# Packing the 256-column chunk of a SwiGLU FFN, and reordering the work around it, in a two-layer decoder trunk

## The chip, the cores and the metric

The kernel runs on one core of one Trainium2 chip. The metric is the device time of one execution in microseconds (us). The engines are called as the profile calls them: PE is TensorE's matmuls, PEld its weight loads, DVE is VectorE, ACT is ScalarE, POOL is GpSimd and SP is SyncE, whose queue issues nearly all DMAs.

## The reference

Two layers of a decoder on 256 positions of width 1024, in fp32. The first layer mixes with a causal gated MLP, the second with a sparse attention of three branches. In both layers the output of the mixer and that of a cross-attention into 256 memory positions are joined and projected, and a SwiGLU FFN of 2816 columns follows:

```python
for i in range(DEPTH):
    h = rmsnorm(x, norm_mix[i]);  mem_n = rmsnorm(mem, norm_mem[i])
    mix, mem_q = gmlp_mixer(h, ...) if i % 2 == 0 else nsa_mixer(h, ...)
    mem_o = mem_cross_attention(mem_q, mem_n, w_mem_kv[i])
    x = x + jnp.concatenate([mix, mem_o], axis=-1) @ w_out
    h = rmsnorm(x, norm_ffn[i])
    x = x + (jax.nn.silu(h @ wg) * (h @ wu)) @ wd
return rmsnorm(x, norm_final)
```

## The kernel before

**Products.** Every fp32 operand of a large product is split into two fp32r parts, high and low: for a weight piece `wH` (a cast on ACT, L123) and `wL` (a subtraction on DVE, L124), for an activation `aH` and `aL` in the same way. `mm3` then issues three matmuls, H·H (L229), L·H (L230) and H·L (L231); such three are called a triple below. The 256 positions are two blocks `tb` of 128. A `gemm` runs the eight 128-row slices of a weight against one block, eight triples into one PSUM tile; `down` runs some slices of a 1024-column weight into `accs[tb][half]`, four PSUM tiles of 512 columns that hold a layer's sum.

**Weights.** All weights pass through one stream: a `Raw` tile is loaded by SP (three buffers), cut into pieces of 1024 columns, and each piece is cast and subtracted into a `wH` and a `wL` of seven buffers. `AHEAD = 7` pieces may be live. A piece is released by `done()` when its last triple is issued, which lets the next be split, and a raw tile is loaded when the pieces of the one three places before it are split. So the order of the calls in the program sets the order of the loads.

**Order.** PE's order is the order of the calls. Between triples `Flow.tick` advances a model clock, and runs generators whose due time (a `spawn` delay or a `yield`) has come; these put transposes and small matmuls between triples. The other engines' instructions are placed by a scheduler, with priorities for what is in a `step`.

**PSUM.** Four tiles `mm` and four tiles `tr`, one bank of 512 columns each. `tr` tiles go round: an instruction that takes one waits until the readers of the tile four places back are done.

**Where the change touches.**

- `ffn_weights` and `ffn` (L429 to L470): the columns are taken as one chunk of 256 and five of 512. In the chunk of 256 the order is `gate(0)`, `up(0)`, `gate(1)`, `up(1)`, each eight triples of 256 columns, and then `down` with two slices. `gate` ends in a silu on ACT (L449), `up` spawns `turn`: the product with the silu on DVE (L453), 1.6 model us later two or four transposes, and the split into `act`, from which `down` reads.
- Layer 1's projection (L695 to L707): `mem_attention` (L382) is spawned for both blocks, the second 5.5 model us after the first. It makes scores (L389), a softmax over DVE, POOL and ACT, `MEMLAT = 9` model us later transposes and two copies on ACT (L414), and 3.2 later the product with the values (L422). The generator `v_chain` transposes the gated product `gm` into the other slices. `down` runs slices 0 to 3, and once both memory blocks are emitted slices 4 to 7 of both blocks.
- Layer 2's attention (L921 to L1073), for six head groups `m`: `scores(m)` leaves probabilities, `turn(m)` transposes them (L973 to L982) and at its end the compressed branch's `pcs` (L984, "tr<-ident,pcx" in the profile, with a copy on ACT at L985), `attend(m)` multiplies with the values (L1003) and splits the result into `mix1`. `mixed((m, tb))` is a `down` of one slice and one block, two triples. All of them stand in a written-out order.
- The end (`final`, L1081): after each 512-column half of a block, the residual (DVE, L307), a sum of squares (ACT, L250), the product with the final norm's weights (DVE, L1087); after a block's second half its factor on POOL (L258, L259) and the two scalings (DVE L1094, ACT L1096), each followed by a DMA of SP (L1097).

Of the kernel before, what the change touches and what calls it, by code (L numbers as in the profile page):

```python
# [12 lines left out]
ALU = mybir.AluOpType  # L13
# [48 lines left out]
MEMLAT = 9.0  # L62
# [6 lines left out]
def body(tc, t, out):  # L69
    nc = tc.nc  # L70
    PE, ACT, DVE, POOL, SP = nc.tensor, nc.scalar, nc.vector, nc.gpsimd, nc.sync
    with ExitStack() as ctx:
# [236 lines left out]
        def down(accs, act, ks, ws, first, last, after=None, tbs=(0, 1)):  # L309

            for tb in tbs:
                for half in range(2):
                    acc = accs[tb][half]
                    for i, k in enumerate(ks):
                        mm3(acc, st(act, k, tb), ws[i](slice(half * 512, (half + 1) * 512)),
                            first and i == 0, last and i == len(ks) - 1)
                        if tb == 1 and half == 1:
                            ws[i].done()
# [110 lines left out]
        def ffn_weights(layer):  # L429
            wg, wu, wd = t["ffn_w_gate"][layer], t["ffn_w_up"][layer], t["ffn_w_down"][layer]  # L430
            out = []
            for c0, n in [(2560, 256)] + [(i * 512, 512) for i in range(5)]:
                out.append((n // 128, w_in(wg, c0, n), w_in(wu, c0, n),
# [3 lines left out]
        def ffn(weights, nrm, after):  # L437
            accs = [[mm(), mm()], [mm(), mm()]]
            for ci, (nk, wg, wu, wd) in enumerate(weights):
                n = nk * 128  # L440
                sil = [None, None]
                act = mid([128, 4, SEQ], F32R), mid([128, 4, SEQ], F32R)

                def gate(tb):
                    ps = tr()
                    gemm(ps, nrm.act, tb, wg, n)
                    sil[tb] = small([128, n])
                    with tc.high_priority(offset=HI):
                        ACT.activation(sil[tb], ps[:, :n], AF.Silu, scale=nrm.rstd[tb])  # L449
# [19 lines left out]
                down(accs, act, range(nk), wd, ci == 0, last, end if last else None)  # L469
# [180 lines left out]
        def v_chain():  # L650
# [17 lines left out]
            for c, n in ((0, 512), (512, 256)):  # L668
                for tb in range(2):
# [4 lines left out]
                    yield 1.0  # L674
# [23 lines left out]
        for tb in range(2):  # L698
            flow.spawn(mem_attention(qT0, tb, kv0, mix, mo_done), 1.0 + 5.5 * tb)
# [270 lines left out]
        def turn(m):  # L970
# [169 lines left out]
```

## Time and profile before

| | us |
|---|---|
| device time, median of 3 runs (lowest, highest) | 633.94 (633.56, 634.37) |
| the profiled execution's own device time | 634.55 |
| its span, first to last instruction | 632.8 |
| PE busy | 618.1 (98%) |
| DVE busy | 377.1 (60%) |
| ACT busy | 327.3 (52%) |
| POOL busy | 58.2 (9%) |
| share of the chain that ended last: PE, ACT, DVE | 90%, 5%, 2% |
| share of 16 DMA engines on the weight queue | 51.9% |

PE's records are pipelined: one begins before the one ahead has ended. So a matmul's price is the distance of its start from the start of the next, and a wait is what such a distance has beyond the usual one. The mean granted clock of the profiled execution was 0.998.

### The profile page before, as it was taken

What the parts mean: (1) busy time and instruction counts of PE and PEld (TensorE: products, weight loads), DVE (VectorE), ACT (ScalarE), POOL (GpSimd) and SP (SyncE); (2) the same over time, 40 slices, a digit from 0 to 9 for tenths busy, and PEclk for the clock granted to TensorE, in tenths of its full rate; (3) what the DMA queues carried; (4) which work ended last, traced back from release to release, by engine and by line L of the source; (5) the groups of instructions that cost most, each with busy time, mean ns of one, the idle gap of its engine ahead of it and who ended that gap; (6) DMA issues with size and microseconds to landing.
All of it is one profiled execution on the core that took longest, in us unless ns stands there. A gap on an engine that the chain in (4) does not pass through costs nothing.

```text
span 632.8 us, 8848 instructions
## 1 busy us (share of the span) xinstructions
PE 618.1 (98%) x3382; PEld 513.9 (81%) x3382; DVE 377.1 (60%) x616; ACT 327.3 (52%) x553; POOL 58.2 (9%) x90
## 2 busy tenths in 40 slices
PE   8999999999999999999999999899999999999995
PEld 7889879888888888889886787678988888888884
DVE  3998457464554544566688479766544645446344
ACT  4885557452534434456543559766533535344423
POOL 0330121000000000002001204431000000000001
PEclk9999999999999999999999999999999999999999
DMA  7966254555546464643967742133554655647401
GB/s 244 369 217 247 75 165 169 200 172 186 177 171 225 138 261 134 241 159 87 330 201 206 193 103 65 35 121 115 198 199 134 226 173 179 220 138 235 159 1 67
DMA packets 57331, 109.69 MB, mean 173 GB/s; under 512 B 3429, under 2 KB 19401, under 8 KB 57289
## 3 DMA queue, kind: packets, MB, share of 16 engines
q1 hardware_dynamic: 57272, 109.12, 51.9%
q8 instruction: 26, 0.43, 0.3%
q14 instruction: 17, 0.13, 0.1%
q10 hardware_dynamic: 16, 0.00, 0.0%
HBM read 108.07 MB, written 1.05 MB: 172 GB/s over the span
## 4 chain that ended last, share of the span: by engine, by line
PE 90%; ACT 5%; DVE 2%; DMA 1%; issue 1%; POOL 0%; SPq 0%; POOLq 0%; ACTq 0%; DVEq 0%
PE mm L229 14%; PE mm L230 14%; PE mm L231 14%; PE tr L230 13%; PE tr L231 13%; PE tr L229 13%; PE tr L245 5%; ACT mid L951 3%; PE tr L800 1%; DMA x<-in_x_dram 1%; PE tr L389 1%; PE tr L422 1%; PE tr L1003 1%; ACT wH L123 1%; DVE wL L124 0%
## 5 line engine op out<-in xcount | busy, mean ns | idle before, releaser
L124 DVE TENSOR_TENSOR wL<-raw,wH 128x1024 fp32r<-128x1024 f32 (+1 forms) x170 | 205.5, 1228 | 149.5 <-ACT wH L123 143.8
L123 ACT CAST wH<-raw 128x1024 fp32r<-128x1024 f32 (+1 forms) x170 | 173.8, 1043 | 152.3 <-PE tr L230 75.5
L229 PE MATMUL tr<-wH,aH 128*128 128x512 f32 (+1 forms) x384 | 143.8, 375 | 0.0
L230 PE MATMUL tr<-wH,aL 128*128 128x512 f32 (+1 forms) x384 | 142.8, 372 | 0.6 <-DVE aL L124 0.6
L231 PE MATMUL tr<-wL,aH 128*128 128x512 f32 (+1 forms) x384 | 142.7, 372 | 0.0
L229 PE MATMUL mm<-wH,aH 128*128 128x512 f32 (+2 forms) x224 | 87.7, 391 | 0.0
L230 PE MATMUL mm<-wH,aL 128*128 128x512 f32 (+2 forms) x224 | 83.2, 371 | 0.0
L231 PE MATMUL mm<-wL,aH 128*128 128x512 f32 (+2 forms) x224 | 83.2, 371 | 0.0
L230 PEld LDWEIGHTS tr<-wH,aL 128*128 128x128 f32 x384 | 72.4, 188 | 13.0 <-DVE aL L124 0.9
L231 PEld LDWEIGHTS tr<-wL,aH 128*128 128x128 f32 x384 | 72.3, 188 | 12.5
L229 PEld LDWEIGHTS tr<-wH,aH 128*128 128x128 f32 x384 | 72.3, 188 | 12.3
L229 PE MATMUL mm<-wH,mid 128*128 128x512 f32 (+1 forms) x208 | 79.2, 381 | 0.0
L230 PE MATMUL mm<-wH,mid 128*128 128x512 f32 (+1 forms) x208 | 77.9, 374 | 0.0
L231 PE MATMUL mm<-wL,mid 128*128 128x512 f32 (+1 forms) x208 | 77.8, 374 | 0.0
L229 PEld LDWEIGHTS mm<-wH,aH 128*128 128x128 f32 x224 | 42.9, 191 | 9.6 <-issue 4.0
L231 PEld LDWEIGHTS mm<-wL,aH 128*128 128x128 f32 x224 | 42.6, 190 | 7.4
L258 POOL TENSOR_SCALAR rstd<-ss 128x1 f32<-128x1 f32 x14 | 8.0, 575 | 434.6 <-ACT junk L250 430.5
L230 PEld LDWEIGHTS mm<-wH,aL 128*128 128x128 f32 x224 | 42.7, 191 | 5.6
L231 PEld LDWEIGHTS mm<-wL,mid 128*128 128x128 f32 x208 | 39.2, 188 | 7.1
L230 PEld LDWEIGHTS mm<-wH,mid 128*128 128x128 f32 x208 | 39.3, 189 | 6.8 <-DVE mid L124 0.5
L229 PEld LDWEIGHTS mm<-wH,mid 128*128 128x128 f32 x208 | 39.2, 189 | 6.7 <-ACT mid L123 0.4
L453 DVE SCALAR_TENSOR_TENSOR small<-tr,rstd,small 128x512 f32<-128x512 f32 (+1 forms) x24 | 16.9, 703 | 36.5 <-PE tr L231 36.5
(158 smaller groups left out, 652.6 us busy)
## 6 DMA issues: line engine op xcount, KB each, us to landing
raw<-in_ffn_w_down_dram SPq DMA_DIRECT2D x22, 1024.0 KB, 5.1
raw<-in_ffn_w_gate_dram SPq DMA_DIRECT2D x20, 1024.0 KB, 5.2
raw<-in_ffn_w_up_dram SPq DMA_DIRECT2D x20, 1024.0 KB, 5.1
raw<-in_nsa_w_in_dram SPq DMA_DIRECT2D x6, 1024.0 KB, 6.9
raw<-in_gmlp_w_in_dram SPq DMA_DIRECT2D x4, 1024.0 KB, 8.1
raw<-in_w_mem_kv_dram SPq DMA_DIRECT2D x4, 1024.0 KB, 5.8
raw<-in_gmlp_w_out_dram SPq DMA_DIRECT2D x4, 1024.0 KB, 6.2
raw<-in_nsa_w_out_dram SPq DMA_DIRECT2D x12, 256.0 KB, 4.9
```

The lines of the kernel that those rows point to most:

```text
L123: ACT.copy(H, src)
L124: DVE.tensor_tensor(L, src, H.bitcast(F32), op=ALU.subtract)
L229: PE.matmul(ps, aH, bH, start=first, stop=False)
L230: PE.matmul(ps, aL, bH, start=False, stop=False)
L231: PE.matmul(ps, aH, bL, start=False, stop=last)
L245: PE.transpose(ps[:, (at + j) * 128 : (at + j + 1) * 128], src[:, j * 128 : (j + 1) * 128], ident)
L258: POOL.tensor_scalar(r, ss[:, 0:1], ss[:, 1:2], EPS, op0=ALU.add, op1=ALU.add)
L389: PE.matmul(scs[i][:, j * 256 : (j + 1) * 256], qT[r, j, :], kv[r, j, :], start=True, stop=True)
L422: PE.matmul(o[i * 64 : i * 64 + 64, blk(j)], kv[:, 2 + b, h : h + 64], pTs[i][:, j * 2 + b, :], start=b == 0, stop=b == 1)
L453: DVE.scalar_tensor_tensor(h, ps[:, :n], nrm.rstd[tb], sil[tb], op0=ALU.mult, op1=ALU.mult)
L800: PE.matmul(ph[s * 64 : s * 64 + 60, 0:256], X[s][:, k // 8, k % 8, :], w1[q, s][:, j, :], start=k == 0, stop=k == 15)
L951: ACT.activation(o, o, AF.Exp, bias=nb[:, i : i + 1], scale=-1.0, accum_out=sm[:, i : i + 1])
```

## The change

**FFN.** In the 256-column chunk gate and up are loaded side by side into one raw tile, [128, 4, 512], by two DMAs each. `gate_up(tb)` runs eight triples of 512 columns and ends in the silu of the left half; `turn` reads the right half, its delay is 2.4. Before `down` the next chunk's `gate` of block 0 is put (eight triples of 512), whose weights are loaded ahead of the down weights.

**Layer 1.** `MEMLAT` is 8 (in both layers), the second `mem_attention` is spawned after 3.5 instead of 5.5, the `gm` transposes 1.0 later. `down` of slices 4 to 7 is cut in three: slices 4 and 5 of block 0 ahead of the memory attention's end, 6 and 7 of block 0 behind it, then 4 to 7 of block 1.

**Layer 2.** The compressed transpose becomes `turn_c(m)`, run behind a `mixed` that used to follow it; the last `mixed` calls have another order.

**The end.** The last half of block 1 is computed in two quarters of 256 columns, each in a `tr` tile of its own; what the sum held before is added to `x` one chunk earlier. The three last scalings go to DVE (two, 256 columns) and ACT (512), and ACT's result is sent by ACT's own queue.

```diff
-MEMLAT = 9.0
+MEMLAT = 8.0
...
+                    if parts and tb == 1 and half == 1:
+                        for j in range(2):
+                            quarter = tr()
+                            for i, k in enumerate(ks):
+                                mm3(quarter[:, 0:256], st(act, k, tb), ws[i](slice(512 + j * 256, 768 + j * 256)),
+                                    i == 0, i == len(ks) - 1)
+                            parts(quarter, j)
...
+                if n == 256:
+                    both = []
+                    for k0 in (0, 4):
+                        loads = []
+                        for j, w in enumerate((wg, wu)):
+                            src = w[k0 * 128 : k0 * 128 + 512, c0 : c0 + n].rearrange("(k p) n -> p k n", p=128)
+                            loads.append((lambda r, j=j: r[:, :, j * 256 : j * 256 + 256], src))
+                        both += Raw([128, 4, 512], loads).kts
+                    ahead = w_in(wg, 0, 512)
...
-                    yield 1.6
+                    yield 1.6 if nk == 4 else 2.4
...
-                for f, tb in ((gate, 0), (up, 0), (gate, 1), (up, 1)) if nk == 2 else ((gate, 0), (gate, 1), (up, 0), (up, 1)):
-                    f(tb)
+                def gate_up(tb):
+                    ps = tr()
+                    gemm(ps, nrm.act, tb, wg, 512)
+                    sil[tb] = small([128, n])
+                    with tc.high_priority(offset=HI):
+                        ACT.activation(sil[tb], ps[:, :n], AF.Silu, scale=nrm.rstd[tb])
+                    flow.spawn(turn(ps[:, n : 2 * n], tb))
+                    flow.tick(0)
+
+                if nk == 2:
+                    for tb in range(2):
+                        gate_up(tb)
+                    gate(ci + 1, 0)
+                else:
+                    for tb in range(1 if ci == 1 else 0, 2):
+                        gate(ci, tb)
+                    for tb in range(2):
+                        up(tb)
...
-                    yield 1.0
+                    yield 2.0
...
-            flow.spawn(mem_attention(qT0, tb, kv0, mix, mo_done), 1.0 + 5.5 * tb)
+            flow.spawn(mem_attention(qT0, tb, kv0, mix, mo_done), 1.0 + 3.5 * tb)
...
+        down(accs, mix, [4, 5], WO0[2], False, False, None, (0,))
         flow.until(lambda: len(mo_done) == 2)
-        down(accs, mix, [4, 5, 6, 7], WO0[2] + WO0[3], False, True,
-             lambda *a: flow.spawn(f0.chain(*a)))
+        after = lambda *a: flow.spawn(f0.chain(*a))
+        down(accs, mix, [6, 7], WO0[3], False, True, after, (0,))
+        down(accs, mix, [4, 5, 6, 7], WO0[2] + WO0[3], False, True, after, (1,))
...
-            tc_ = tr()
-            transposes(tc_, pcs[:, m % 2], 1)
-            ACT.copy(pcT[:, m % 2], tc_[:, 0:128])
             turned[m] = pT0, pT1
+
+        def turn_c(m):
+            t = tr()
+            transposes(t, pcs[:, m % 2], 1)
+            ACT.copy(pcT[:, m % 2], t[:, 0:128])
...
         step(turn, 3)
         mixed((0, 1))
+        step(turn_c, 3)
         step(scores, 5)
         mixed((2, 0))
         step(attend, 3)
         step(turn, 4)
-        mixed((1, 1), (3, 0))
+        mixed((1, 1))
+        step(turn_c, 4)
+        mixed((3, 0))
         step(attend, 4)
         step(turn, 5)
-        mixed((2, 1), (4, 0))
+        mixed((2, 1))
+        step(turn_c, 5)
         step(attend, 5)
-        mixed((3, 1), (5, 0), (4, 1), (5, 1))
+        mixed((4, 0), (5, 0), (3, 1), (4, 1), (5, 1))
...
+        def last(quarter, j):
+
+            c = slice(512 + j * 256, 768 + j * 256)
+            xs = x[:, 1, c]
+            DVE.tensor_tensor(xs, quarter[:, 0:256], xs, op=ALU.add)
+            sumsq(xs, sst[j], D)
...
+            if j == 1:
+                r = tiny([128, 1], "rstd")
+                POOL.tensor_tensor(r, sst[0], sst[1], op=ALU.add)
+                POOL.tensor_tensor(r, r, neghalf, op=ALU.pow)
+                xa, xb, xc = xgs[-3:]
+                DVE.tensor_scalar(xc, xc, r, None, op0=ALU.mult)
+                ACT.activation(xa, xa, AF.Copy, scale=r)
+                SP.dma_start(oview[:, 1, c], xc)
+                DVE.tensor_scalar(xb, xb, r, None, op0=ALU.mult)
+                ACT.dma_start(oview[:, 1, 0:512], xa)
+                SP.dma_start(oview[:, 1, 512:768], xb)
```

**Three places of the order.** A changed line number behind the same operation is the same call in the changed file (L422 becomes L432, L414 L424, L976, L982 and L985 become L1019, L1025 and L1031).

PE in layer 1's projection, before: the transposes of the two memory blocks ("ident,small") and their products with the values (L422).

```order
L245 MATMUL tr<-ident,small 128x128 x8
L229 MATMUL mm<-wH,aH 128x512
L230 MATMUL mm<-wH,aL 128x512
L231 MATMUL mm<-wL,aH 128x512
L422 MATMUL tr<-small,memkv 64x128 x8
L245 MATMUL tr<-ident,small 128x128 x8
L422 MATMUL tr<-small,memkv 64x128 x8
```

The same place after; the first block's transposes stand five triples above.

```order
L245 MATMUL tr<-ident,small 128x128 x8
L432 MATMUL tr<-small,memkv 64x128 x8
L229 MATMUL mm<-wH,aH 128x512
L230 MATMUL mm<-wH,aL 128x512
L231 MATMUL mm<-wL,aH 128x512
L229 MATMUL mm<-wH,aH 128x512
L230 MATMUL mm<-wH,aL 128x512
L231 MATMUL mm<-wL,aH 128x512
L432 MATMUL tr<-small,memkv 64x128 x8
```

Between a block's transposes and its product stood one triple, or nothing; now it is five triples with eight transposes, or one product with two triples.

ACT at the end of layer 2's attention, before, with buffer numbers: `turn(4)` ends in the copy L985 of `tr_4037`, a weight cast follows, then the split of `attend(4)`, `turn(5)` with the copy of `tr_4098`, a cast, and the split of `attend(5)`.

```order
L985 COPY pcx_3413<-tr_4037 128x128
L123 CAST wH_4049<-raw_3591 128x1024
L123 CAST aH_2650<-tr_4058 128x256
L976 COPY mid_4082<-tr_4077 128x512
L982 COPY mid_4089<-tr_4084 128x512
L982 COPY mid_4096<-tr_4091 128x512
L985 COPY pcx_3413<-tr_4098 128x128
L123 CAST wH_4110<-raw_3723 128x1024
L123 CAST aH_2650<-tr_4119 128x256
```

The same place after.

```order
L123 CAST wH_3997<-raw_3371 128x1024
L1031 COPY pcx_3362<-tr_3991 128x128
L123 CAST aH_2598<-tr_4004 128x256
L1019 COPY mid_4028<-tr_4023 128x512
L1025 COPY mid_4035<-tr_4030 128x512
L1025 COPY mid_4042<-tr_4037 128x512
L123 CAST wH_4075<-raw_3371 128x1024
L1031 COPY pcx_3362<-tr_4050 128x128
L123 CAST aH_2598<-tr_4053 128x256
```

The copy that `attend` reads has gone from ahead of the weight cast to behind it.

PE in layer 2's first FFN chunk, after, with buffer numbers: the second block's transposes of `turn`, in the midst of the next chunk's gate (`tr_4267`), to the first triple of `down`.

```order
L245 MATMUL tr_4280<-ident_85,small_4261 128x128 x2
L229 MATMUL tr_4267<-wH_4161,aH_3443 128x512
L230 MATMUL tr_4267<-wH_4161,aL_3444 128x512
L231 MATMUL tr_4267<-wL_4162,aH_3443 128x512
...
L229 MATMUL tr_4267<-wH_4223,aH_3443 128x512
L230 MATMUL tr_4267<-wH_4223,aL_3444 128x512
L231 MATMUL tr_4267<-wL_4224,aH_3443 128x512
L229 MATMUL mm_4150<-wH_4240,mid_4154 128x512
L230 MATMUL mm_4150<-wH_4240,mid_4155 128x512
L231 MATMUL mm_4150<-wL_4241,mid_4154 128x512
```

Before, these transposes stood in `down` itself, one triple ahead of the first that reads what they lead to; now four triples stand between.

## Rows read from the trace of the kernel before

**Rows 1.** The page: the span, and PE's busy time, share and instructions.

```profile
span 632.8 us, 8848 instructions
PE 618.1 (98%) x3382; PEld 513.9 (81%) x3382; DVE 377.1 (60%) x616; ACT 327.3 (52%) x553; POOL 58.2 (9%) x90
```

**Rows 2.** Waits of PE: line, releaser, us in total, times, longest us.

```profile
PE tr L245 <- DVE aL L124: 2.5, 3, 1.0
...
PE tr L245 <- DVE small L673: 0.2, 1, 0.2
```

**Rows 3.** Timeline of PE, layer 2: start, duration (us), line, tiles, count.

```profile
432.81 0.39 PE L230 MATMUL mm<-wH,aL 128*128 128x512 f32 x1
...
435.76 0.39 PE L231 MATMUL mm<-wL,aH 128*128 128x512 f32 x1
...
449.30 0.28 PE L231 MATMUL tr<-wL,aH 128*128 128x256 f32 x1
...
451.82 0.28 PE L231 MATMUL tr<-wL,aH 128*128 128x256 f32 x1
```

**Rows 4.** Timeline of PE, layer 2, first FFN chunk, where `down` follows `turn`.

```profile
454.93 0.43 PE L229 MATMUL mm<-wH,mid 128*128 128x512 f32 x1
455.32 0.50 PE L230 MATMUL mm<-wH,mid 128*128 128x512 f32 x1
455.65 0.39 PE L231 MATMUL mm<-wL,mid 128*128 128x512 f32 x1
```

**Rows 5.** Waits of PEld, 83 to 89 us; then PE's timeline.

```profile
PEld tr L422 <- ACT small L414: 1.7, 4, 0.6
...
84.09 1.57 PE L422 MATMUL tr<-small,memkv 128*64 128x128 f32 x16
...
354.86 1.09 PE L422 MATMUL tr<-small,memkv 128*64 128x128 f32 x16
```

**Rows 6.** Timeline of PE, layer 2: the compressed transposes and their waits.

```profile
395.94 0.33 PE L245 MATMUL tr<-ident,pcx 128*128 128x128 f32 x1 [0.55 <-ACT mid L976]
...
403.95 0.33 PE L245 MATMUL tr<-ident,pcx 128*128 128x128 f32 x1 [0.99 <-DVE aL L124]
...
411.77 0.33 PE L245 MATMUL tr<-ident,pcx 128*128 128x128 f32 x1 [1.00 <-DVE aL L124]
...
420.63 0.33 PE L245 MATMUL tr<-ident,pcx 128*128 128x128 f32 x1 [0.48 <-DVE aL L124]
```

**Rows 7.** Timeline of PE at the entry to layer 2's FFN.

```profile
438.52 0.28 PE L229 MATMUL tr<-wH,aH 128*128 128x256 f32 x1
439.37 0.39 PE L230 MATMUL tr<-wH,aL 128*128 128x256 f32 x1 [0.58 <-DVE aL L124]
```

**Rows 8.** Timeline of ACT, layer 2: a weight cast between two attention steps.

```profile
428.38 1.05 ACT L123 CAST wH<-raw 128x1024 fp32r<-128x1024 f32 x1 [0.35 <-PE mm L230]
```

**Rows 9.** Groups by line and shape: count | busy us, mean ns | idle.

```profile
L124 DVE TENSOR_TENSOR aL<-tr,aH 128x256 fp32r<-128x256 f32 x12 | 5.0, 416 | 6.1 <-ACT aH L123 6.1
...
L453 DVE SCALAR_TENSOR_TENSOR small<-tr,rstd,small 128x256 f32<-128x256 f32 x4 | 1.9, 479 | 1.1 <-PE tr L231 1.1
...
L449 ACT ACTIVATE small<-tr,rstd 128x256 f32<-128x256 f32 x4 | 1.9, 472 | 0.0
...
L250 ACT ACTIVATE junk<-Vv 128x256 bf16<-128x256 f32 x2 | 0.8, 417 | 0.0
```

**Rows 10.** End of the chain that ended last: start, duration (us), line.

```profile
626.13 0.70 DVE x L307
...
626.91 0.73 ACT junk L250 x2
...
627.74 0.30 POOL rstd L258
...
628.70 0.72 ACT small L1096
```

**Rows 11.** The page's DMA issues: count, KB each, us from issue to landing.

```profile
raw<-in_ffn_w_gate_dram SPq DMA_DIRECT2D x20, 1024.0 KB, 5.2
```

More of the change, by code (lines that the diff above doesn't have):

```diff
@@ L307, in residual, with down @@
             DVE.tensor_tensor(xs, acc, xs, op=ALU.add)
-        def down(accs, act, ks, ws, first, last, after=None, tbs=(0, 1)):
+        def down(accs, act, ks, ws, first, last, after=None, tbs=(0, 1), parts=None, ends=False):
             for tb in tbs:
@@ L313, in down @@
                     acc = accs[tb][half]
+                    if parts and tb == 1 and half == 1:
[5 more added lines that the diff above has]
+                            parts(quarter, j)
+                        for w in ws:
+                            w.done()
+                        continue
                     for i, k in enumerate(ks):
                         mm3(acc, st(act, k, tb), ws[i](slice(half * 512, (half + 1) * 512)),
-                            first and i == 0, last and i == len(ks) - 1)
+                            first and i == 0, (last or (ends and tb == 1 and half == 1)) and i == len(ks) - 1)
                         if tb == 1 and half == 1:
@@ L432, in ffn_weights, with ffn, gate @@
             for c0, n in [(2560, 256)] + [(i * 512, 512) for i in range(5)]:
-                out.append((n // 128, w_in(wg, c0, n), w_in(wu, c0, n),
+                if n == 256:
[7 more added lines that the diff above has]
+                    ahead = w_in(wg, 0, 512)
+                out.append((n // 128, both if n == 256 else ahead if c0 == 0 else w_in(wg, c0, n),
+                            None if n == 256 else w_in(wu, c0, n),
                             sum([cols(wd, c0 // 128 + k, 2, 0, D) for k in range(0, n // 128, 2)], [])))
             return out
-        def ffn(weights, nrm, after):
+        def ffn(weights, nrm, after, parts=None):
             accs = [[mm(), mm()], [mm(), mm()]]
+            sils = [[None, None] for _ in weights]
+            def gate(ci, tb):
+                ps = tr()
+                gemm(ps, nrm.act, tb, weights[ci][1], 512)
+                sils[ci][tb] = small([128, 512])
+                with tc.high_priority(offset=HI):
+                    ACT.activation(sils[ci][tb], ps, AF.Silu, scale=nrm.rstd[tb])
             for ci, (nk, wg, wu, wd) in enumerate(weights):
                 n = nk * 128
-                sil = [None, None]
+                sil = sils[ci]
                 act = mid([128, 4, SEQ], F32R), mid([128, 4, SEQ], F32R)
[L444 to L449, printed above, removed]
                 def turn(ps, tb, act=act, sil=sil, n=n, nk=nk):
@@ L1018, in step @@
         def step(f, *a):
-            with tc.high_priority(offset=UP if f is turn else HI):
+            with tc.high_priority(offset=UP if f in (turn, turn_c) else HI):
                 f(*a)
@@ L1099, in final @@
             yield
+        def last(quarter, j):
[3 more added lines that the diff above has]
+            sumsq(xs, sst[j], D)
+            if j == 0:
+                POOL.tensor_scalar(sst[0], sst[0], sse[1][:, 0:1], EPS, op0=ALU.add, op1=ALU.add)
+            xg = small([128, 256])
+            DVE.tensor_tensor(xg, xs, nf[:, c], op=ALU.mult)
+            xgs.append(xg)
+            if j == 1:
[9 more added lines that the diff above has]
+                SP.dma_start(oview[:, 1, 512:768], xb)
         xgs = []
-        ffn(WF1, f1, final)
-        flow.until(lambda: len(xgs) == 4)
+        ffn(WF1, f1, final, last)
+        flow.until(lambda: len(xgs) == 5)
 _INS = [
```

11 lines of the change are left out of this document (10 added, 1 removed).

## The prediction

> **What bounds the kernel now.** I read the page first: PE is busy for 618.1 of a span of 632.8 us [rows 1]. DVE and ACT are busy for half of it, and the weight queue's transfers for about the same. So the kernel is bound by PE, and time can come from two places only: fewer or cheaper matmuls, and the stretches in which PE stands still. Second, the timeline of PE gives the price of a matmul, by starts. From 432.81 to 435.76 us lie 13 distances of matmuls of 512 columns, 0.227 us each; from 449.30 to 451.82 lie 21 of 256 columns, 0.120 us each [rows 3]. A triple of 512 is thus 0.68 us. Third, the waits of PE say where it stands still: the largest entry is 2.5 us in three waits of transposes for an `aL` of DVE [rows 2]. The timeline shows these and others one by one: four compressed transposes [rows 6], the entry to layer 2's FFN [rows 7], the turn into `down` in the first chunk of each FFN [rows 4], and the products of layer 1's memory attention with the values [rows 5]. Last, the chain that ended last shows what runs when PE is done: residual, sum of squares, factor and scaling, one behind the other [rows 10].
>
> The sum is made against the profiled execution, 634.55 us, of which the span is 632.8 and 1.75 lies around it. The median of the three runs is 633.94, so that execution is 0.61 us long, and I take 0.61 off at the end.
>
> **The change part by part.**
>
> *Packing.* A layer's chunk had 32 triples of 256 columns and gets 16 of 512 in their place: 48 times two matmuls of 0.120 become one of 0.227 us. Each saves 0.013, so 48 × 0.013 = 0.62 us per layer, 1.25 in both. The eight triples of the next gate are moved, not added. The weights are the same bytes in the same number of pieces; SP issues four DMAs for two raw tiles where it issued four for four. The Trainium skill (page "TensorE: Matmul & The Clock Gate", section "Wait — 56ns, not 53.3ns?") states a fixed cost of about 2.5 ns per matmul beside its columns, by which the saving would be 48 × 2.5 ns = 0.12 us per layer, an estimate from that page. The rows stand against it: by them the fixed part is five times as large, and I take the rows.
>
> *Turn into down.* In the old order one triple stands between the second block's transposes and the `down` matmuls that read their split. The first two of these cost 0.39 and 0.33 us to the next start [rows 4], 0.16 and 0.10 over the pace, 0.26 together; layer 1 shows the same. With four triples of the next gate (2.7 us) behind the transposes this goes: 0.52 in both layers. What must fit under the cover is ACT's cast and DVE's subtraction of 256 columns (about 0.42 each [rows 9]), with a weight cast of 1.05 [rows 8] ahead of them if it comes badly: 1.9, less than 2.7. Ahead of the transposes stand the silu, 0.47, and the product, 0.48 [rows 9]. Before, the silu had long been done when the product came; now both follow one gemm, again under four triples: 0.95 and a cast, 2.0 against 2.7. I cost this new chain at nothing; without the cover it costs up to one cast, 1.05 us, per turn.
>
> *Layer 1's projection.* PE's weight loads of the two value products wait 1.7 us for ACT's copies, in four waits, and the sixteen records of such a product last 1.57 us where layer 2's unhindered ones last 1.09 [rows 5]. Now five triples (3.4 us) and eight transposes stand behind the first block's transposes, and one product and two triples (2.4 us) behind the second's. The two copies take a bit over one us, with a weight cast ahead 2.1. So most of the 1.7 goes. I take 1.4, since the second cover is thin; the bounds are 0 and 1.7. The softmax ahead of it now has less time (`MEMLAT` 8, second block two model us earlier), and what is late next is POOL's scaling of the second block, which I hold to be just in time. The `gm` transposes, one model us later, can save at most the 0.2 us that one of them waits for DVE [rows 2]; I take 0, since what follows may wait in its place.
>
> *Compressed transposes.* The four wait 0.55, 0.99, 1.00 and 0.48 us [rows 6]. They take the `tr` tile that `attend` has filled, so they come free when DVE has read it. Behind a `mixed` they come 1.4 us or more later. But two of these `mixed` read the `aL` that is just being made, so there the wait only moves to the second matmul: of the first I count 0, of the second 0.3. The third and fourth `mixed`, (0,1) and (1,1), read older ones: 1.0 and 0.5. Together 1.8, with bounds 1.0 and 3.0. Against this, `turn_c(5)` is followed by `attend(5)`, which reads its copy, and ACT's order shows a weight cast between `mixed((2,1))` and that copy. The cast takes 1.05 us [rows 8]; it starts when the piece comes free, early in the `mixed`, and I count a new wait of 0.7 (bounds 0 and 1.3, a cast with its copy). Net gain 1.1.
>
> *Entry to layer 2's FFN.* The first matmul on the new `aL` starts 0.85 us after the one before it [rows 7], 0.73 over the 0.120 pace. The transposes were followed by two triples; now by four, 1.36 us more cover. DVE has one weight subtraction ahead of the split there, so I count the 0.73 as just covered. Bounds 0 and 0.8.
>
> *The end.* Two quarters are 24 matmuls of 0.120, 2.88 us, where the half had 12 of 0.227, 2.72: 0.16 more. Behind the last matmul the residual (0.70 for 512 columns [rows 10]) is on 256 columns, for which the nearest row is 0.42 [rows 9]: 0.28 less. The sum of squares takes 0.73 with its read-out [rows 10]; on 256 columns the nearest row of ACT is 0.417 without it [rows 9], to which I add a tenth for what of the read-out shows: 0.2 less. POOL's two instructions stay two (0.30 for the first [rows 10]). The last scaling is ACT's on 512 columns as before, 0.72. Net 0.32; I take 0.3, with bounds −0.1 (POOL's new form dearer, three DMAs where there were two) and 0.6. The Trainium skill ("DMA: Bandwidth & Descriptors", "Issuing engines are not separate DMA queues") says that issuing from a second engine saves only the issue time, since all share the same DMA engines; so I count nothing for the ACT queue's DMA.
>
> Sum: 1.25 + 0.52 + 1.4 + 0 + 1.1 + 0.73 + 0.3 = 5.3 us. 634.55 − 5.3 = 629.25; less 0.61 for the median: 628.6 us.
>
> **The rivals.**
>
> *The waits only move* (attention and FFN entry). For it: two of four `mixed` read the `aL` in question, and ACT is dense there. Against it: the others don't. If only 0.4 of 1.8 is left: 630.0 us.
>
> *The packed chunk's chains are late.* For it: silu and product now stand in a row behind one gemm, and ACT casts weights all the time. Against it: 2.7 us of cover. At one cast per layer lost at a turn, 2.1: 630.7 us; at all four turns 632.8.
>
> *Only the packing acts.* The model clock's delays may move steps without freeing PE. Then 1.25 + 0.52 is all: 632.2 us.
>
> *The page's price of a matmul.* By it the packing gives 1.0 us less: 629.6. The mechanism would be that the 0.120 of 256 columns is not the matmul's own but that of the weight load beside it; PEld runs beside PE in either form, so I give it little. That page's rule hangs on no other term.
>
> *Slower: the weight stream starves.* The next gate's four pieces are now held from ahead of `down` to behind it, and with the two of `down` they leave one of seven live pieces for what follows. A raw tile lands 5.2 us after its issue [rows 11] and is cast in 1.05 [rows 8]. The second `gate_up` and the next gate are 16 triples, 10.9 us; two landings one behind the other are 10.4. If the down weights wait for both and come behind them, PE stands for a landing and a cast, 6.25 us, in each layer: in one layer 633.94 − 5.3 + 6.25 = 634.9 us, in both 641.1. For it: the small margin. Against it: three raw buffers let landings overlap, and PE waits for no weight piece in the trace of before. It decides from the point at which a landing takes over 5.4 us with no overlap.
>
> **How the numbers follow.** Chances: forecast 0.70, waits only move 0.11, late chains 0.08, only packing 0.04, the page's price 0.02, starved stream 0.05. The lower bound comes from the bounds of the terms: 1.7 for layer 1, 0.2 for `gm`, 1.9 for the attention and 0.6 for the end add 1.6, which gives 627.0. The upper reaches over the first two rivals, and over a forecast that lacks layer 1's 1.4, to 631.3. A measurement of this kernel tells about 0.2%, 1.27 us, from no change. The forecast and most of the first two rivals are beyond that, and only packing (1.8 us) just so; same or slower needs the starved stream or several terms at their worst: faster 0.91, same 0.05, slower 0.04.
>
> **What would show it.** In PE's rows: no matmul of 256 columns in the first chunk of an FFN, 48 of 512 columns at 0.227 instead; no distance above 0.25 at the first `down` matmuls; value products in layer 1 of 1.1 us; compressed transposes without a wait but for the second; a wait of 0.7 us for the copy in `attend(5)`; no gap at the entry to layer 2's FFN; and about 2.2 us from the last matmul to the last scaling. Wrong would be a PE wait on a `wH` or `wL` in the first chunks, a PE wait for a silu or a `turn`, or a new wait in the softmax of layer 1's second block.

## The result and the profile after

The changed kernel takes 627.89 us (median of 4 runs, 627.38 to 628.40) against 633.75 us of the kernel before (4 runs, 633.00 to 634.37). The ratio is 0.9908, with a 95% interval of 0.9891 to 0.9925: 4.7 to 6.9 us less. The forecast was 628.6. The profiled execution of the changed kernel took 628.40 us, its span 626.7; those of [rows 1] are 634.55 and 632.8.

The page shows PE as the bound still, with 2.4 us less of its own work; the group by shape shows where that comes from. The kernel before had 64 matmuls of L229 with 256 columns on `tr<-wH,aH` and 320 with 512; the former are gone, and of the latter there are 352.

```profile
span 626.7 us, 8677 instructions
...
PE 615.7 (98%) x3298; PEld 508.7 (81%) x3298; DVE 375.6 (60%) x620; ACT 328.4 (52%) x555; POOL 60.3 (10%) x91
```

```profile
L229 PE MATMUL tr<-wH,aH 128*128 128x512 f32 x352 | 138.5, 393 | 0.0
```

The waits of PE in the changed kernel (columns as in [rows 2]) no longer hold the compressed transposes. What is left is `x` at the start, a `mq` of layer 1 (the memory queries, which DVE makes late), two `mixed` that wait for an `aL`, the wait of the scores for a `mid` (L970, 0.5 us), which the kernel before has too, and the copy of the compressed transpose (L1031).

```profile
PE tr L245 <- DMA x<-in_x_dram: 0.9, 2, 0.6
PE tr L245 <- DVE small L734: 0.8, 1, 0.8
PE mm L230 <- DVE aL L124: 0.7, 2, 0.4
PE tr L970 <- ACT mid L1019: 0.5, 1, 0.5
PE tr L1048 <- ACT pcx L1031: 0.4, 1, 0.4
```

To see where the 6.1 us between the two profiled spans lie, I cut both timelines of PE at the same matmuls:

| stretch on PE, start to start (us) | before | after | less |
|---|---|---|---|
| start to the first matmul of layer 1's projection | 69.40 | 68.81 | 0.59 |
| to the first matmul of layer 1's FFN | 31.50 | 30.04 | 1.46 |
| to the first turn of that FFN's second chunk | 36.54 | 35.81 | 0.73 |
| to the first matmul behind that FFN | 151.06 | 151.11 | −0.05 |
| to the first scores of layer 2's attention | 89.11 | 88.63 | 0.48 |
| to the first matmul of layer 2's FFN | 60.91 | 59.77 | 1.14 |
| to the first turn of that FFN's second chunk | 37.77 | 36.35 | 1.42 |
| to the last matmul's start | 149.42 | 149.70 | −0.28 |
| to the end of the span | 7.10 | 6.47 | 0.63 |

All but the first and the fifth are steady: three profiles of the changed kernel agree in each of them within 0.04 us. The first differs by more than a microsecond from one execution to the next, since it hangs on when the pieces of `x` land and on the wait for `mq` (below). So I compare kernels below by the time from the projection's first matmul to the end of the span, "from the projection on": 563.41 us in the first profile of before, 557.87 after.

**The first FFN chunk** in layer 2, where [rows 4] showed 0.39 and 0.33 us between starts. The second turn's transposes now stand in the next gate, four triples ahead, and the `down` matmuls start 0.22 to 0.23 apart.

```profile
449.10 0.44 PE L245 MATMUL tr<-ident,small 128*128 128x128 f32 x2
449.29 0.48 PE L229 MATMUL tr<-wH,aH 128*128 128x512 f32 x1
449.61 0.40 PE L230 MATMUL tr<-wH,aL 128*128 128x512 f32 x1
...
452.15 0.39 PE L229 MATMUL mm<-wH,mid 128*128 128x512 f32 x1
452.37 0.39 PE L230 MATMUL mm<-wH,mid 128*128 128x512 f32 x1
452.60 0.39 PE L231 MATMUL mm<-wL,mid 128*128 128x512 f32 x1
```

**Layer 1's value products**, 1.57 us for sixteen records in [rows 5], are as short as layer 2's.

```profile
85.52 1.09 PE L432 MATMUL tr<-small,memkv 128*64 128x128 f32 x16
...
88.13 1.09 PE L432 MATMUL tr<-small,memkv 128*64 128x128 f32 x16
```

**The compressed transposes** of [rows 6] wait for nothing. But the first two waits stand in the `mixed` now: its second matmul, which reads `aL`, starts 0.80 and 0.92 us after the first. The third and the fourth are gone, with a new one behind the third: the last scores (L974) last from 409.46 to 411.13, 1.67 us where the kernel before took 1.04. And `attend(5)` waits for the copy L1031 of `turn_c(5)`.

```profile
392.25 0.50 PE L229 MATMUL mm<-wH,aH 128*128 128x512 f32 x1
393.05 0.50 PE L230 MATMUL mm<-wH,aL 128*128 128x512 f32 x1 [0.30 <-DVE aL L124]
...
399.75 0.49 PE L229 MATMUL mm<-wH,aH 128*128 128x512 f32 x1
400.67 0.50 PE L230 MATMUL mm<-wH,aL 128*128 128x512 f32 x1 [0.43 <-DVE aL L124]
...
408.55 0.27 PE L245 MATMUL tr<-ident,pcx 128*128 128x128 f32 x1
...
409.46 1.75 PE L974 MATMUL tr<-KT,QT 64*128 64x512 f32 x4
411.13 0.50 PE L229 MATMUL mm<-wH,aH 128*128 128x512 f32 x1
...
424.87 0.44 PE L1048 MATMUL tr<-pcx,vc 128*64 128x128 f32 x4 [0.37 <-ACT pcx L1031]
```

ACT's timeline shows what that copy stood behind: the weight cast, as its order foretold. The longer scores have the same cause. PE's weight loads wait there for the copy L1031 of `turn_c(3)`, since the last of the four `tr` tiles that the scores take is the one which that copy has to empty; and the copy stood behind a weight cast too.

```profile
410.08 0.29 PEld L974 LDWEIGHTS tr<-KT,QT 64*128 64x128 f32 x2 [0.35 <-ACT pcx L1031]
```

```profile
408.82 1.05 ACT L123 CAST wH<-raw 128x1024 fp32r<-128x1024 f32 x1
409.76 0.27 ACT L1031 COPY pcx<-tr 128x128 f32<-128x128 f32 x1
...
423.61 1.04 ACT L123 CAST wH<-raw 128x1024 fp32r<-128x1024 f32 x1 [0.41 <-PE mm L230]
424.56 0.26 ACT L1031 COPY pcx<-tr 128x128 f32<-128x128 f32 x1
```

**The entry to layer 2's FFN**, 0.85 us in [rows 7], is at the pace of 512 columns.

```profile
434.16 0.39 PE L229 MATMUL tr<-wH,aH 128*128 128x512 f32 x1
434.39 0.39 PE L230 MATMUL tr<-wH,aL 128*128 128x512 f32 x1
```

**The end**, to be held against [rows 10]: residual 0.44 for 0.70, sum of squares 0.52 for 0.73, POOL and the last scaling much as before. From the residual's start to the scaling's end it is 2.74 us where it was 3.29.

```profile
620.54 0.44 DVE x L1158
...
621.05 0.52 ACT junk L250 x2
...
621.71 0.19 POOL rstd L1167
...
622.56 0.72 ACT small L1171
```

### The profile page after: what moved, and what is told of

Read it like the earlier page. It is cut to its first block, busy times and chain, and to the rows that moved or that the text cites. A ratio compares the mean times of both kernels' runs of the same rounds, so it can differ in the third digit from the quotient of the medians.

```text
span 626.7 us, 8677 instructions
## 1 busy us (share of the span) xinstructions
PE 615.7 (98%) x3298; PEld 508.7 (81%) x3298; DVE 375.6 (60%) x620; ACT 328.4 (52%) x555; POOL 60.3 (10%) x91
## 4 chain that ended last, share of the span: by engine, by line
PE 87%; ACT 4%; DMA 4%; DVE 3%; issue 1%; SPq 0%; POOL 0%; POOLq 0%; ACTq 0%
PE mm L229 13%; PE tr L231 13%; PE tr L229 13%; PE tr L230 13%; PE mm L230 13%; PE mm L231 13%; PE tr L245 5%; ACT mid L994 2%; DMA raw<-in_gmlp_w_in_dram 1%; DMA x<-in_x_dram 1%; PE tr L1048 1%; PE tr L843 1%; DMA raw<-in_w_mem_kv_dram 1%; DVE wL L129 1%; ACT wH L128 1%
## 5 line engine op out<-in xcount | busy, mean ns | idle before, releaser
L229 PE MATMUL tr<-wH,aH 128*128 128x512 f32 x352 | 138.5, 393 | 0.0
L231 PE MATMUL tr<-wL,aH 128*128 128x512 f32 x352 | 137.2, 390 | 0.0
L230 PE MATMUL tr<-wH,aL 128*128 128x512 f32 x352 | 137.1, 389 | 0.0
L229 PE MATMUL mm<-wH,aH 128*128 128x512 f32 (+2 forms) x224 | 87.3, 390 | 0.1
L229 PE MATMUL mm<-wH,mid 128*128 128x512 f32 (+1 forms) x204 | 77.5, 380 | 0.0
L231 PEld LDWEIGHTS tr<-wL,aH 128*128 128x128 f32 x352 | 66.1, 188 | 13.9
L230 PEld LDWEIGHTS tr<-wH,aL 128*128 128x128 f32 x352 | 66.1, 188 | 13.4
L229 PEld LDWEIGHTS tr<-wH,aH 128*128 128x128 f32 x352 | 66.1, 188 | 13.3
L231 PE MATMUL mm<-wL,mid 128*128 128x512 f32 (+1 forms) x204 | 76.2, 374 | 0.0
L230 PE MATMUL mm<-wH,mid 128*128 128x512 f32 (+1 forms) x204 | 76.0, 373 | 0.0
L229 PEld LDWEIGHTS mm<-wH,aH 128*128 128x128 f32 x224 | 42.5, 190 | 10.3 <-issue 4.0
L230 PEld LDWEIGHTS mm<-wH,mid 128*128 128x128 f32 x204 | 38.5, 189 | 6.4
L229 PEld LDWEIGHTS mm<-wH,mid 128*128 128x128 f32 x204 | 38.4, 188 | 6.3
```

The lines of the kernel that those rows point to most:

```text
L229: PE.matmul(ps, aH, bH, start=first, stop=False)
L230: PE.matmul(ps, aL, bH, start=False, stop=False)
L231: PE.matmul(ps, aH, bL, start=False, stop=last)
```

## The experiments

Twelve runs followed, each with the kernel before beside it: the changed kernel twice more, the kernel before once more, and nine variants of the changed kernel. This is the time from the projection's first matmul to the end of the span in each profile, and the ratio of the run times to the kernel before on the same chip.

| run | from the projection on (us) | ratio, 95% interval |
|---|---|---|
| before, first and second profile | 563.41, 563.12 | 1 |
| changed, first profile | 557.87 | 0.9908 (0.9891, 0.9925) |
| c1_again, c3_again (the changed kernel) | 557.93, 558.11 | 0.9903 (0.9885, 0.9921), 0.9908 (0.9896, 0.9921) |
| e1_layer1_back | 559.38 | 0.9935 (0.9918, 0.9952) |
| e2_latency_back_l2 | 558.08 | 0.9911 (0.9891, 0.9930) |
| e3_compressed_back | 558.81 | 0.9925 (0.9908, 0.9943) |
| e4_chunk_back | 560.28 | 0.9945 (0.9930, 0.9959) |
| e5_no_gate_under | 561.14 | 0.9955 (0.9939, 0.9971) |
| e6_attend5_later | 558.08 | 0.9916 (0.9903, 0.9929) |
| e7_copy_on_dve | 558.75 | 0.9924 (0.9911, 0.9937) |
| e8_lag | 560.25 | 0.9943 (0.9928, 0.9957) |
| e9_lag_and_dve | 559.76 | 0.9941 (0.9928, 0.9954) |

**The two kernels once more.** c1_again and c3_again are the changed kernel, c2_before the one before, without an edit.

> The changed kernel once more, as the measure for the three beside it. In its first profile PE is 1.19 us ahead of the kernel before at the mask products of layer 1, before anything that the change touches, and at the first matmul of layer 1's projection 0.59 ahead. Theory: that lead is a matter of when x lands at the start, not of the change, so it differs here (a wait for x anywhere between 0.9 and 1.7 us) while all stage lengths from layer 1's projection on repeat within 0.1 us, and the ratio to the kernel before is 0.991. Rival: the lead belongs to the change (another order of loads at the start), and the wait for x is 0.9 us again.

> The kernel before, for a second profile. In the first one PE reached the mask products of layer 1 at 55.98 us, the five of the changed kernel and its variants lie between 53.64 and 54.79, and twelve transposes of layer 2's memory attention took 1.79 us where all others take 1.42. Theory: both belong to that one execution (x lands at another time; an issue wait), so this profile reaches that point anywhere from 53.5 to 56, and the twelve transposes take 1.4; from the first matmul of layer 1's projection to the end it is 0.4 us shorter than 563.41. Rival: both belong to the kernel and are seen again.

> The changed kernel as the measure for the three beside it: from the first scores of layer 2 to its first FFN matmul 59.8 us as in both profiles of it so far, ratio to before about 0.991.

The changed kernel reached the projection at 68.81, 67.57 and 67.76 us, the kernel before at 69.40 and 68.15. The waits for `x`, 0.9, 2.0 and 2.0 us in the changed kernel, do not measure this: the executions that waited longer came earlier. What does is when the third of the four loads of `x` landed (10.46, 9.72 and 10.03 us) and how long PE then waited for `mq` (0.8, 0.2 and 0.2 us); the two together give the differences between the three within 0.05 us. The wait for `x` was short in the first profile because PE was still at work: from 8.06 us on its matmuls of 512 columns started 0.42 to 0.43 us apart, in c1_again 0.24 to 0.34, with a granted clock of 1.00 in the rows of both. Why they were slower is not shown. The lead of 0.59 is thus no part of the change that I could show: both kernels range over more. Of the stretch ahead of layer 2's scores, the second profile of before has 88.77, 0.34 less than the first. In the first, the last four of the twelve transposes of the memory attention waited 0.28 us for nothing that the profile shows ("issue"); in the second the row has no such wait, and they take 1.43 us in all instead of 1.79. The first and the second profile of before:

```profile
349.46 1.12 PE L245 MATMUL tr<-ident,small 128*128 128x128 f32 x8
350.86 0.63 PE L245 MATMUL tr<-ident,small 128*128 128x128 f32 x4 [0.28 <-issue]
```

```profile
348.19 1.67 PE L245 MATMUL tr<-ident,small 128*128 128x128 f32 x12
```

So the change is worth 5.0 to 5.5 us from the projection on, by these five profiles. The three sets of runs put the medians 5.9, 6.1 and 5.6 us apart, a little more in each; whether some of that belongs to the change ahead of the projection is not shown.

**e1: layer 1's projection as before.**

```diff
-                    yield 2.0
+                    yield 1.0
...
-            flow.spawn(mem_attention(qT0, tb, kv0, mix, mo_done), 1.0 + 3.5 * tb)
+            flow.spawn(mem_attention(qT0, tb, kv0, mix, mo_done, 9.0), 1.0 + 5.5 * tb)
...
-        down(accs, mix, [4, 5], WO0[2], False, False, None, (0,))
         flow.until(lambda: len(mo_done) == 2)
-        after = lambda *a: flow.spawn(f0.chain(*a))
-        down(accs, mix, [6, 7], WO0[3], False, True, after, (0,))
-        down(accs, mix, [4, 5, 6, 7], WO0[2] + WO0[3], False, True, after, (1,))
+        down(accs, mix, [4, 5, 6, 7], WO0[2] + WO0[3], False, True,
+             lambda *a: flow.spawn(f0.chain(*a)))
```

> The changed kernel with layer 1's projection as before (memory latency 9 and spacing 5.5 in layer 1, gm transposes 1.0, down of slices 4 to 7 in one piece). Theory: the change's gain there is the wait for ACT's two copies, 1.45 us by the traces from the first projection matmul to the first FFN matmul, so this takes 1.4 to 1.5 us more than the changed kernel (ratio to before about 0.993), the value products wait again 1.7 us in four waits, and nothing later gives any of it back. Rival: the softmax chain over DVE, POOL and ACT bounds the stretch, and the waits only stand elsewhere in the changed order: then under 0.5 us more.

The stretch from the projection to the FFN is 31.54 us again, 1.50 longer, and from the projection on the kernel takes 1.4 us more. The waits of the weight loads for ACT's copies between 78 and 92 us are back as in [rows 5]:

```profile
PEld tr L432 <- ACT small L424: 1.7, 4, 0.6
```

Nothing later gave any of it back. The softmax chain wasn't the bound. The run puts the latency, the spacing, the `gm` delay and the cut of `down` back together; which of them carries the gain is not told apart.

**e2: the memory attention's latency of layer 2 back to 9**, by an argument of `mem_attention` (`9.0` in its two calls of layer 2).

> The changed kernel with the memory attention's latency 9 instead of 8 in layer 2 alone. The prediction gave this nothing; the traces show 0.48 us less from the second compressed-key stretch to the scores. Theory: the latency moves a value product's transposes past a wait of 0.45 us, so this run is 0.4 to 0.5 us slower than the changed kernel, and the wait of a transpose for an ACT result stands in the trace again near the twelve transposes. Rival: the 0.48 comes from somewhere else (what the shift of everything by 2.7 us did to the DMAs), and the trace of this run has the stretch as short as the changed kernel.

A miss of the theory: 558.08 us, within the spread of the changed kernel, and the stretch ahead of the scores is 88.75 where that kernel has 88.63 to 88.79. The latency does nothing there. With c2_before the 0.48 is explained: 0.34 was that one execution, and 0.1 is within what the other profiles show.

**e3: the compressed transposes back at the end of each turn**, the six `step(turn_c, m)` taken out, the last `mixed` in the changed order.

```diff
             turned[m] = pT0, pT1
-        def turn_c(m):
-            t = tr()
-            transposes(t, pcs[:, m % 2], 1)
-            ACT.copy(pcT[:, m % 2], t[:, 0:128])
+            tc_ = tr()
+            transposes(tc_, pcs[:, m % 2], 1)
+            ACT.copy(pcT[:, m % 2], tc_[:, 0:128])
```

> The changed kernel with the compressed transposes at the end of each turn again, all else, the last order of the projection steps too, as changed. Theory: by the stages the move won 1.2 at the third, 0.65 at the fourth, 0.2 at the second, and lost 0.1 at the first, 0.66 in scores 5 and 0.5 in attend 5: net 0.7 to 1.1 us, so this run is that much slower than the changed kernel, with waits of 0.5, 1.0, 1.0 and 0.5 us back at the compressed transposes and no wait for the copy in attend 5. Rival: the waits for DVE's aL are a bound of the DVE and ACT chains from scores to attend, the move won nothing net and the 1.15 us come from the last order alone: then within 0.3 us of the changed kernel.

The attention's stretch is 60.65 us for 59.77 to 59.81, 0.84 to 0.88 more, with the four old waits in PE's timeline and none at the last transpose:

```profile
391.50 0.33 PE L245 MATMUL tr<-ident,pcx 128*128 128x128 f32 x1 [0.55 <-ACT mid L1019]
...
399.52 0.33 PE L245 MATMUL tr<-ident,pcx 128*128 128x128 f32 x1 [0.99 <-DVE aL L124]
...
407.33 0.33 PE L245 MATMUL tr<-ident,pcx 128*128 128x128 f32 x1 [0.99 <-DVE aL L124]
...
416.18 0.33 PE L245 MATMUL tr<-ident,pcx 128*128 128x128 f32 x1 [0.47 <-DVE aL L124]
```

So the move is worth 0.86, and the last order the rest of 1.14, about 0.3, which no run shows by itself.

**e4: the 256-column chunk of both FFNs as before.**

```diff
-                        gate_up(tb)
-                    gate(ci + 1, 0)
+                        gate(ci, tb)
+                        up(tb)
...
-                    for tb in range(1 if ci == 1 else 0, 2):
+                    for tb in range(2):
```

(with the weights' loads and the turn's delay as they were).

> The changed kernel with the 256-column chunk of both FFNs as before: 32 triples of 256 columns, gate and up in turn, no next gate under it. Theory: the chunk won 0.7 us per layer by the stage lengths (layer 1 from the first FFN matmul to the second chunk's first turn 36.54 to 35.81, less at layer 2), so this run is 1.4 us slower than the changed kernel, with the 0.39 and 0.33 us starts back at the second block's down; the entry to layer 2's FFN stays without its wait, since the order ahead of it is as changed. Rival: the entry's 0.73 us belong to the chunk (a triple of 512 columns in its place covers more than one of 256), and this run is over 2 us slower.

The stretch with layer 1's chunk is 36.53 us for 35.81, that with layer 2's 37.05 for 36.35: 0.72 and 0.70, as expected, and the entry to layer 2's FFN keeps its gain. But the run is 2.3 us slower, not 1.4: 0.89 us more stand in layer 1's projection (30.93 for 30.04), where nothing was edited. ACT's timeline shows why. With four raw tiles for the chunk instead of two, a cast in ACT's order needs a tile whose transfer was issued late (at 82.31 us, landed at 86.65), and waits 1.30 us for it; the splits of the memory attention are behind it in that queue, and PE's weight loads wait 0.9 us for the `aL`:

```profile
86.73 1.05 ACT L123 CAST wH<-raw 128x1024 fp32r<-128x1024 f32 x1 [1.30 <-DMA raw<-in_ffn_w_up_dram]
87.68 0.37 ACT L123 CAST aH<-tr 128x256 fp32r<-128x256 f32 x1
```

```profile
PEld mm L230 <- DVE aL L124: 0.9, 1, 0.9
```

The new order of layer 1's projection and the packed chunk thus need each other: with the old chunk's loads the new order is worth 0.57 us (31.50 less 30.93), with the new ones 1.46; and the new loads alone are worth nothing there (31.54 in e1).

**e5: packed, but no gate under the turn, and its delay 1.6.**

```diff
-                    gate(ci + 1, 0)
...
-                    yield 1.6 if nk == 4 else 2.4
+                    yield 1.6
```

> The changed kernel with gate and up packed, but without the next chunk's gate ahead of down, and with the old delay of 1.6 for the turn. Theory: the packing alone is worth its matmuls, 0.6 us per layer less what the switches between transposes and matmuls take, and the gate under it only the wait at down, 0.26 per layer, so this run is 0.3 to 0.7 us slower than the changed kernel. Rival: the packed silu and product stand behind one gemm, so that without the gate the second turn is late by the silu, the product and a cast: 1 to 2 us per layer slower, and the packing without it would have been a loss.

The rival was right: 1.63 and 1.60 us more in the two stretches. Packed columns without the next gate are slower than the old chunk (37.44 us against 36.54 in layer 1), and the 0.62 of cheaper matmuls is more than eaten. (The gate and the turn's longer delay were taken out together; the packed chunk with another delay alone was not tried.) ACT's timeline shows the first cause in layer 2: ahead of the first silu stands a load of its table, 1.28 us. Ahead of the second stands a weight cast, and on DVE the subtraction of the same piece, which holds the product until 449.50, 0.8 us after that silu has ended.

```profile
441.22 1.28 ACT L491 ACT_TABLE_LOAD   x1 [1.92 <-PE tr L231]
...
447.27 1.06 ACT L123 CAST wH<-raw 128x1024 fp32r<-128x1024 f32 x1 [0.32 <-PE tr L230]
448.23 0.47 ACT L491 ACTIVATE small<-tr,rstd 128x256 f32<-128x256 f32 x1
```

```profile
448.36 1.23 DVE L124 TENSOR_TENSOR wL<-raw,wH 128x1024 fp32r<-128x1024 f32 x1
449.50 0.48 DVE L474 SCALAR_TENSOR_TENSOR small<-tr,rstd,small 128x256 f32<-128x256 f32 x1
```

The transposes of both turns wait for the product that follows; the starts ahead of them are 0.78 and 1.01 us apart, from 442.79 and 449.11:

```profile
443.57 0.44 PE L245 MATMUL tr<-ident,small 128*128 128x128 f32 x2 [0.39 <-DVE small L474]
...
450.12 0.41 PE L245 MATMUL tr<-ident,small 128*128 128x128 f32 x2 [0.63 <-DVE small L474]
```

The rest is the old 0.26 at `down`.

**e6: attend 5 behind mixed (4,0).**

```diff
+        mixed((4, 0))
         step(attend, 5)
-        mixed((4, 0), (5, 0), (3, 1), (4, 1), (5, 1))
+        mixed((5, 0), (3, 1), (4, 1), (5, 1))
```

> The changed kernel with mixed (4,0) between the last compressed transpose and attend 5, instead of behind attend 5. Theory: attend 5 waits 0.54 us for the copy that is queued behind a weight cast on ACT; with two more triples (1.4 us) between, the copy is done, and this run is 0.5 us faster than the changed kernel (ratio to before about 0.990). Rival: the wait moves to mixed (5,0), which reads attend 5's result 1.4 us earlier than now: then no gain, with the wait for aL standing there.

The rival was right. `attend(5)` no longer waits, but `mixed((5,0))` right behind it does, for the `aH` of its result, and the stretch is 59.97 us.

```profile
428.37 0.50 PE L229 MATMUL mm<-wH,aH 128*128 128x512 f32 x1 [0.47 <-ACT aH L123]
```

**e7, e8, e9: attempts to take the waits that are left.** e7 puts the copy on DVE; e8 moves each projection step one place later; e9 does both.

```diff
-            ACT.copy(pcT[:, m % 2], t[:, 0:128])
+            DVE.tensor_copy(pcT[:, m % 2], t[:, 0:128])
```

```diff
-        mixed((6, 1), (7, 1))
+        mixed((6, 1))
         step(turn, 0)
...
-        mixed((0, 0))
+        mixed((7, 1))
         step(turn_c, 1)
...
-        mixed((1, 0))
+        mixed((0, 0))
         step(turn_c, 2)
...
-        mixed((2, 0))
+        mixed((1, 0))
...
-        mixed((3, 0))
+        mixed((2, 0))
...
         step(turn_c, 5)
+        mixed((3, 0))
         step(attend, 5)
```

> The changed kernel with the copy of the compressed transposes on DVE instead of ACT. Theory: the two new waits of layer 2 are ACT's queue (0.5 us in attend 5 for the copy behind a weight cast, 0.6 in scores 5 for the copy behind two turn copies), so both go and the stretch from scores to FFN takes 58.7 to 59.2 us where the changed kernel takes 59.8. Rival: DVE's chain from scores to attend is as dense there, the copy delays the reduction or the aL behind it, and the stretch stays within 0.2 us.

> The changed kernel with every projection step of layer 2 one place later, so that none of them reads the aL that is just being made: mixed (7,1), (0,0), (0,1) behind the turns 1 to 3, (3,0) ahead of attend 5. Theory: the wait at the first and second compressed transpose only moved into the projection step's second matmul (0.58 and 0.70 us beyond the pace in the profile after); with an older operand there it goes, and the stretch is 1.2 us shorter, plus 0.3 to 0.5 for attend 5: 58.1 to 58.6. Rival: what those waits cover is the scores chain, and the time comes back as a wait of scores 3 and 4 for their PSUM tiles or of the next attend: then under 0.4 us.

> Both of the last two together. Theory: 1.5 to 2.2 us shorter than the changed kernel in the stretch (57.6 to 58.3), ratio to before about 0.988. Rival: the two take the same waits away, and it is no better than the better of them.

All three are slower than the changed kernel, a loss that none of the expectations foresaw: 60.59, 62.14 and 61.62 us in the stretch, for 59.8. In e7 `attend(5)` is free of its wait, but the scores of step 2 now wait 0.80 us for the copy in DVE's queue, and those of step 5 are as long as in the changed kernel (1.65 us), since their weight loads wait for the same copy, now on DVE:

```profile
388.81 1.55 PE L974 MATMUL tr<-KT,QT 64*128 64x512 f32 x4 [0.80 <-DVE pcx L1031]
```

In e8 the waits of the two `mixed` for `aL` are gone, but the turn of step 1 comes two triples earlier, ahead of its probabilities: its transposes wait 2.2 us for POOL's scaling, which idles until 388.79 for what comes from DVE.

```profile
PE tr L245 <- POOL mid L999: 2.2, 2, 1.7
```

```profile
388.79 4.81 POOL L999 TENSOR_TENSOR mid<-mid,f 128x256 f32<-128x256 f32 x6 [3.87 <-DVE mxc L1004]
```

There the chain from scores over DVE, ACT and POOL to the turn bounds the first steps; e9 has the same wait for POOL, 1.9 us. No version was found that beats the changed kernel. One with the copy on DVE for `m = 5` alone, where e7 gained, was not tried.

## Why the prediction was right

The time, 627.89 us, is 0.7 us below the forecast and within the range; the direction was the likely one. By steps, in us:

- *Packing and turn into down*, 1.77 foretold, 1.43 measured (0.73 and 0.70, confirmed by e4). The wait at `down` went as described. The missing 0.34 stands in small pieces. The second turn's transposes come 0.07 us late in each layer, those of `x` in layer 2 (435.88) take 0.12 more, and the rest is spread over many starts. The 0.32 us behind the transposes at 449.10 is no part of it: the last transpose is followed after 0.03 instead of 0.11 us, so that the two starts together keep the pace, and the kernel before has the same pair. The step that was badly argued is the cover: I counted silu and product at nothing, with 2.0 us of chain under 2.7 of cover. It all but holds in the changed kernel, by less than I wrote. In layer 2 the table load of 1.28 us that opens this row wasn't in my sum:

```profile
440.91 1.28 ACT L492 ACT_TABLE_LOAD   x1 [1.92 <-PE tr L231]
```

```profile
442.71 0.48 DVE L475 SCALAR_TENSOR_TENSOR small<-tr,rstd,small 128x256 f32<-128x256 f32 x1 [2.04 <-ACT small L492]
...
448.56 0.48 DVE L475 SCALAR_TENSOR_TENSOR small<-tr,rstd,small 128x256 f32<-128x256 f32 x1
```

The product is ready 0.2 us ahead of the first turn's transposes (443.39) and 0.05 ahead of the second's. e5 shows the price without that cover, and there the rival of late chains is what happens. The Trainium skill ("ScalarE activation tables: per-element evaluation and per-set limits", section "What a function is on this engine") gives 1283 ns for such a load; the trace agrees with 1.28.
- *Layer 1's projection*, 1.4 foretold, 1.46 in the profiles, 1.50 by e1. I did not see that it depends on the chunk's loads (e4).
- *The `gm` transposes*, 0 foretold. A transpose near them waits for `mq` of DVE instead (0.8 us in the profile after, 0.2 to 1.5 in the eleven profiles with this order; the wait for `gm` is 0.2 to 0.5 in the three with the old). The stretch ahead of the projection differs more between executions than such an effect; this stays open.
- *Compressed transposes*, net 1.1 foretold, 1.14 measured, but with other parts. Step by step on PE's timeline: the first won 0.06 with the scores behind it (0 foretold), the second 0.17 (0.3), the third 1.21 (1.0), the fourth 0.65 (0.5). Scores 5 lost 0.66: the mechanism that I foretold for `attend(5)`, a copy behind a weight cast, at a place where I had not looked for it. From `attend(5)` to the FFN 0.29 was lost (0.7 foretold): the product takes 0.6 more with its wait, and the transposes of `x` behind it 0.26 less. The sum was right by luck: gains larger by 0.3 and a loss at `attend(5)` smaller by 0.4 met an unseen loss of 0.66.
- *Entry to layer 2's FFN*, 0.73 foretold. The stretch that holds it lost 1.42, of which the chunk is 0.70 by e4: 0.72.
- *The end*, 0.3 foretold, 0.35 measured (0.63 less 0.28 for the quarters' matmuls). No run put the old end back; this is read from the profiles alone.

Together 5.3 foretold; measured 1.43 + 1.46 + 1.14 + 0.72 + 0.35 = 5.1 on the path from the projection on. The medians differ by 5.86, with an interval that holds both; the rest is ahead of the projection, where the profiles spread, or noise. The starved weight stream did not come about: no PE wait for a weight piece stands in the profile after. The Trainium skill's price of a matmul, 2.5 ns beside the columns ("TensorE: Matmul & The Clock Gate", "Wait — 56ns, not 53.3ns?"), is not borne out here: by it and the 0.26 at `down` a layer's chunk would have won 0.38, and e4 shows 0.70 to 0.72.

## What to carry to other kernels

A saving in matmuls is worth what the chain behind them leaves: here packed columns without the next gate lost 0.9 us per layer, and the work put under the chain (the next gate) turned that into a gain of 0.7. An engine's queue couples steps that share no data, so a reorder has to be read with the loads and casts that stand in the same queue; under the old chunk's loads the projection's gain was 0.57 us instead of 1.46. Before taking a wait away, ask which chain ends next: four further attempts (e6 to e9) each took a wait away and met one as long or longer.

## What was not expected

The start of an execution differs by up to two microseconds before the first layer is half done: the fourteen profiles reach the projection between 67.46 and 69.50 us, while all later stretches but the one ahead of layer 2's scores repeat within 0.07 us for the same order. In c1_again, c3_again and the first profile after, the landing of `x` and one wait for DVE make up the differences. In that spread a gain of 0.5 us can be read from a profile's stretches, but hardly from run times.
